# Expert SwiGLU in split float32: one weight tile in six multiplied unsplit for experts with few tokens

## The chip, the cores and the metric

The kernel runs on one core of a Trainium2 chip. The metric is the device time of one execution in microseconds. Before the change it is 1894.84 us, the median of three runs (1893.42 to 1896.1).

## The reference

Two layers of a decoder over 272 tokens (16 meta tokens and 256 of the sequence), all in float32. Each layer has a mixer and a channel mixer; the second layer's channel mixer is the one that matters here: top-2-of-8 experts, each a SwiGLU.

```
logits = t @ router_w + router_b            # (256, 8)
combine = softmax of the top 2, else 0
for e in range(8):
    gate, up = split(t @ w_gu[e])           # 1024 -> 2 x 3584
    out += combine[:, e] * ((silu(gate) * up) @ w_down[e])   # 3584 -> 1024
```

## The kernel before

TensorE has a fast form of float32 product that keeps fewer bits (float32r). For full precision the kernel writes each weight and each activation as a sum of a high part, rounded to float32r, and a low part, the rest, and adds three fast products: high by high, high by low, low by high.

Two thirds of the way, after both mixers and the dense channel mixer, comes the expert stage (`experts`). The tokens of an expert are gathered into a tile `xe` that holds their high and low parts side by side; up to 128 tokens of one expert fit. An expert is worked in 7 steps of 512 hidden columns (56 steps for 8 experts). A step has six units, each one weight tile of 128 x 2048 float32 (1 MB), in the order up 0, up 1, down 0, down 1, up 2, up 3. Up 0 and up 1 make the gate's 512 columns, up 2 and up 3 the up projection's; down 0 and down 1 belong to the step two before. For each unit:

- SP loads the tile into one of 11 buffers (`raw`, line 1228), as soon as the buffer is free.
- ACT copies it, rounded, to `mhi` (`make_high`, line 1241): the high split. There are 3 such buffers. It stands two units ahead of PE in the program.
- DVE subtracts, `raw` minus `mhi`, to `wlo` (`make_low`, line 1250): the low split, one unit ahead of PE, 3 buffers.
- PE multiplies (`products`). An expert with more than 64 tokens (called full here) takes 12 matmuls of 128 x 512: 8 with `mhi` (line 1262, the tokens' high and low parts apart), 4 with `wlo` (line 1264). An expert with up to 64 tokens (called light) has its high and low token parts side by side in one stationary operand of 128 columns (`both`), and takes 8: 4 with `mhi`, 4 with `wlo`. Which arm is taken is a branch on PE alone (line 1271), on a register loaded from the tile `fulli` (line 1289).

Between the units stand small operations. ACT evicts the gate's and the up projection's sums from PSUM (`evict`, line 1294); PE transposes them in quarters (`turn`, line 1300); ACT copies one half of a transposed tile (`second`, line 1304) and DVE adds the other (`total`, line 1308); ACT takes silu of the gate (line 1312), DVE multiplies with the up part (`product`, line 1315), and ACT and DVE split the result for the down projection (`inner`, lines 1326 and 1328). In an expert's second and third step the sums of the expert before are combined into the output (lines 1351, 1353, 1359, 1365), and in odd experts the gathering of the next two experts is strewn in.

The stage runs in the order in which it is written (`manual_schedule`); each engine works its list in order, and the tags that follow `slot` say where each piece stands. The low split of the next step's up 0 stands in slot 5, behind `inner` and ahead of `total` of the gate.

Of the kernel before, what the change touches and what calls it, by code (L numbers as in the profile page):

```python
# [2 lines left out]

# [1 line left out]

# [10 lines left out]
AF = mybir.ActivationFunctionType  # L16
# [45 lines left out]
def rr(ap):  # L62
    return ap.bitcast(F32)
# [38 lines left out]
class Builder:  # L102
# [974 lines left out]
    def some(self, name, shape, dt=F32):  # L1077

        return self.tmp("rt_" + name, shape, dt, bufs=1)
# [125 lines left out]
    def expert_units(self):  # L1205


        self.steps = [(e, j) for e in range(N_EXPERTS) for j in range(NJ)]
        n = len(self.steps)
        self.units = []  # L1210
        for i in range(n):
            self.units += [("up", i, 0), ("up", i, 1)]
            if i > 1:
                self.units += [("down", i - 2, 0), ("down", i - 2, 1)]
            self.units += [("up", i, 2), ("up", i, 3)]
        self.units += [("down", i, q) for i in (n - 2, n - 1) for q in range(2)]
        self.raws, self.high, self.low, self.whole = [], [], [], {}

    def load_unit(self):
        if len(self.raws) == len(self.units):  # L1220
# [10 lines left out]
    def pieces(self, k):  # L1231
        n = 1024 if k == len(self.units) - 1 else 2048
        return [slice(c, c + n) for c in range(0, 2048, n)]

    def make_high(self, k):

        if k < len(self.high) or k >= len(self.units):
            return
        hi = self.hip.tile([P, 2048], F32R, tag="mhi", name=self.name("mhi"))
        for v in self.pieces(k):  # L1240
            self.nc.scalar.activation(hi[:, v], self.raws[k][:, v], AF.Copy)  # L1241
        self.whole[k] = hi
        self.high.append([hi[:, c : c + 512] for c in range(0, 2048, 512)])

    def make_low(self, k):
        if k < len(self.low) or k >= len(self.units):
            return
        lo = self.wp.tile([P, 2048], F32R, tag="w", name=self.name("wlo"))
        for v in self.pieces(k):
            self.nc.vector.tensor_sub(lo[:, v], self.raws[k][:, v], rr(self.whole[k][:, v]))  # L1250
        self.low.append([lo[:, c : c + 512] for c in range(0, 2048, 512)])
        self.load_unit()

    def products(self, k, full, parts, first, last):


        mm = self.nc.tensor.matmul

        def some(cases):
            for i, ((ps, x), hv) in enumerate(zip(parts, self.high[k])):  # L1260
                for c, a in enumerate(cases(x)):
                    mm(ps, a, hv, start=i in first and c == 0, stop=False)  # L1262
            for i, ((ps, x), lv) in enumerate(zip(parts, self.low[k])):
                mm(ps, cases(x)[0], lv, start=False, stop=i in last)  # L1264

        whole = lambda x: (x[:, 0, :], x[:, 1, :])
        both = lambda x: (x.rearrange("p a n -> p (a n)")[:, 0 : 2 * P : 2],)
        if full is None:
            some(whole)
        else:  # L1270
            with self.tc.If(full > 0) as case:
                some(whole)
            with case.Else():
                some(both)

    def experts(self, base, first):

# [3 lines left out]
        nc = self.nc  # L1281
        V, ACT = nc.vector, nc.scalar.activation
        steps = self.steps
        fulls, ps, g, f2, py, y2, sums = {}, {}, {}, {}, {}, {}, {}
        split4 = lambda x: x.rearrange("p (q h n) -> p q h n", h=2, n=HALF)

        def value(e):
            if e < N_EXPERTS:
                fulls[e] = None if base else nc.values_load(
                    self.fulli[0:1, e : e + 1], engines=[mybir.EngineType.PE], min_val=0, max_val=1)  # L1290

        def evict(i, half):
            g[i, half] = self.tmp(f"e{half}", [P, 512], bufs=2 - half)
# [76 lines left out]
        if base == 0:  # L1370
            self.route_end()
        with self.tc.manual_schedule():
            value(0)
            value(1)
            k = 0
            while len(self.raws) < 11:
# [4 lines left out]
            for i, (e, j) in enumerate(steps):  # L1381
# [3 lines left out]
                if j == 2:  # L1385
                    value(e + 1)
# [58 lines left out]
            last = len(steps) - 1  # L1445
# [15 lines left out]
        e = N_EXPERTS - 1  # L1461
# [189 lines left out]
```

## Time and profile before

| | |
|---|---|
| median of three runs | 1894.84 us |
| the profiled execution | 1896.18 us, span 1894.5 us |
| mean granted TensorE clock | 0.984 of full |
| busy: PE, PEld, DVE, ACT, POOL | 94%, 82%, 81%, 68%, 16% |
| DMA | 497.11 MB, mean 262 GB/s |
| first to last expert matmul | 897.8 to about 1874 us |

Busy shares of a whole span mix stages. From about 900 us on the kernel is in the expert stage, where DMA moves 312 to 405 GB/s until the stage's last slice. Which engine ends the waits there has to be read step by step.

### The profile page before, as it was taken

The page shows a single profiled execution, that of the slowest core. Times are in us where ns is not written, and L with a number is a line of the kernel's source. Part 1 is how long each engine was busy: PE and PEld are TensorE (multiplying, and loading weights), DVE is VectorE, ACT ScalarE, POOL GpSimd, SP SyncE. Part 2 cuts the span into 40 slices and gives each one's busy share as a digit, 9 for nine tenths or more (in the row PEclk, how much of TensorE's full clock was granted, in tenths as well). Part 3 has the DMA queues.
Part 4 walks back from the last instruction along what each step waited for, and adds up shares of the span by engine and source line. Part 5 has one row for each costly group of instructions (what it writes and reads, how often), then busy time and mean ns, then how long its engine had stood idle before and what let it go on. Part 6 is the DMA issues. An engine that isn't in the chain of part 4 may idle for free.

```text
span 1894.5 us, 28350 instructions
## 1 busy us (share of the span) xinstructions
PE 1774.5 (94%) x10763; PEld 1545.1 (82%) x10763; DVE 1541.4 (81%) x1700; ACT 1290.0 (68%) x1649; POOL 310.2 (16%) x385
## 2 busy tenths in 40 slices
PE   8999999899999999998999888899999988888996
PEld 7989999899999999997787666677788866666784
DVE  7796665855577967756889999998889899999987
ACT  5564554644456755654788888887777888888774
POOL 6115721600131247423000000000000000000000
PEclk8999999999999999998999999999999999999998
DMA  5445545354454455565799999999899999999990
GB/s 207 147 146 174 176 163 169 106 185 165 155 206 146 153 173 196 185 215 207 279 359 377 360 353 378 390 402 326 312 352 348 363 355 364 394 360 405 366 353 25
DMA packets 74836, 497.11 MB, mean 262 GB/s; under 512 B 9340, under 2 KB 10924, under 8 KB 17324
## 3 DMA queue, kind: packets, MB, share of 16 engines
q1 hardware_dynamic: 69200, 486.64, 69.5%
q10 hardware_dynamic: 5468, 8.15, 1.5%
q8 instruction: 115, 1.88, 0.4%
q14 instruction: 53, 0.43, 0.1%
HBM read 493.65 MB, written 1.10 MB: 261 GB/s over the span
## 4 chain that ended last, share of the span: by engine, by line
PE 65%; DVE 17%; ACT 6%; issue 5%; DMA 5%; POOL 2%; DVEq 0%; ACTq 0%; SPq 0%; POOLq 0%
PE ps_mm L199 12%; PE ps_mm L200 12%; PE ps_mm L201 12%; DVE wlo L1250 11%; PE ps_mm L1262 10%; PE ps_mm L1264 6%; PE ps_acc L1262 4%; DMA raw<-in_up 4%; ACT mhi L1241 4%; PE ps_acc L1264 2%; PE ps_tp L1300 1%; DVE e L1308 1%; PE ps_acc L535 1%; DVE w L173 1%; PE ps_acc L608 1%
## 5 line engine op out<-in xcount | busy, mean ns | idle before, releaser
L1250 DVE TENSOR_TENSOR wlo<-raw,mhi 128x2048 fp32r<-128x2048 f32 x336 | 759.5, 2280 | 56.3 <-ACT mhi L1241 56.3
L1241 ACT ACTIVATE mhi<-raw 128x2048 fp32r<-128x2048 f32 x336 | 633.3, 1908 | 27.3 <-PE ps_acc L1262 17.6
L173 DVE TENSOR_TENSOR w<-raw,w 128x1024 fp32r<-128x1024 f32 (+2 forms) x261 | 322.0, 1234 | 167.1 <-ACT w L172 166.0
L199 PE MATMUL ps_mm<-HL,w 128*128 128x272 f32 (+2 forms) x1344 | 392.5, 292 | 2.0 <-DVE t L394 1.7
L200 PE MATMUL ps_mm<-HL,w 128*128 128x272 f32 (+2 forms) x1344 | 385.3, 287 | 1.1 <-DVE HL L378 1.1
L201 PE MATMUL ps_mm<-HL,w 128*128 128x272 f32 (+2 forms) x1344 | 385.8, 287 | 0.0
L1262 PE MATMUL ps_mm<-mhi,xe 128*128 128x512 f32 x1336 | 354.5, 401 | 1.3 <-issue 1.3
L172 ACT ACTIVATE w<-raw 128x1024 fp32r<-128x1024 f32 (+2 forms) x262 | 267.3, 1020 | 123.9 <-PE ps_mm L201 89.5
L1264 PE MATMUL ps_mm<-wlo,xe 128*128 128x512 f32 x892 | 253.1, 406 | 44.0 <-DVE wlo L1250 43.7
L1262 PEld LDWEIGHTS ps_mm<-mhi,xe 128*128 128x128 f32 x1336 | 250.0, 192 | 53.7 <-issue 4.1
L199 PEld LDWEIGHTS ps_mm<-HL,w 128*128 128x128 f32 x1344 | 253.3, 188 | 5.1 <-issue 3.2
L200 PEld LDWEIGHTS ps_mm<-HL,w 128*128 128x128 f32 x1344 | 253.1, 188 | 1.7 <-DVE HL L378 1.3
L201 PEld LDWEIGHTS ps_mm<-HL,w 128*128 128x128 f32 x1344 | 253.0, 188 | 0.3 <-DVE w L173 0.2
L1264 PEld LDWEIGHTS ps_mm<-wlo,xe 128*128 128x128 f32 x892 | 167.5, 194 | 104.1 <-DVE wlo L1250 72.4
L1262 PE MATMUL ps_acc<-mhi,f 128*128 128x512 f32 x672 | 178.6, 400 | 0.2 <-DVE f L1328 0.2
L1545 POOL TENSOR_TENSOR raw<-raw,gb 128x768 f32<-128x768 f32 x1 | 1.8, 1802 | 985.9 <-ACT raw L1535 985.9
L1262 PEld LDWEIGHTS ps_acc<-mhi,f 128*128 128x128 f32 x672 | 123.5, 190 | 23.8 <-DVE f L1328 0.5
L1294 ACT ACTIVATE e<-ps_mm 128x512 f32<-128x512 f32 x112 | 66.8, 596 | 95.9 <-PE ps_mm L1264 94.2
L1264 PE MATMUL ps_acc<-wlo,f 128*128 128x512 f32 x448 | 126.6, 404 | 4.8 <-DVE wlo L1250 3.4
L1264 PEld LDWEIGHTS ps_acc<-wlo,f 128*128 128x128 f32 x448 | 82.5, 192 | 36.4 <-DVE wlo L1250 21.7
L493 POOL TENSOR_SCALAR seg<-b,ctm 128x16 f32<-128x16 f32 (+3 forms) x96 | 101.0, 1071 | 41.5 <-PE ps_acc L535 20.6
L200 PE MATMUL ps_mm<-YS,w 128*128 128x272 f32 (+1 forms) x256 | 73.2, 286 | 0.0
(355 smaller groups left out, 2477.3 us busy)
## 6 DMA issues: line engine op xcount, KB each, us to landing
raw<-in_up SPq DMA_DIRECT2D x224, 1024.0 KB, 7.0
raw<-in_down SPq DMA_DIRECT2D x110, 1024.0 KB, 7.2
raw<-in_g SPq DMA_DIRECT2D x24, 1024.0 KB, 4.9
raw<-in_q SPq DMA_DIRECT2D x12, 1024.0 KB, 5.4
raw<-in_x SPq DMA_DIRECT2D x12, 1024.0 KB, 4.8
raw<-in_dg SPq DMA_DIRECT2D x11, 1024.0 KB, 4.9
raw<-in_du SPq DMA_DIRECT2D x11, 1024.0 KB, 4.8
raw<-in_dd SPq DMA_DIRECT2D x16, 704.0 KB, 4.0
```

What stands on the lines that cost most here:

```text
L172: pin(nc.scalar.activation(hv, src, AF.Copy))
L173: pin((eng or nc.vector).tensor_sub(lv, src, rr(hv)))
L199: nc.tensor.matmul(ps, h, a, start=first and k == 0, stop=False)
L200: nc.tensor.matmul(ps, h, b, start=False, stop=False)
L201: nc.tensor.matmul(ps, lo, a, start=False, stop=last and k == kn - 1)
L493: nc.gpsimd.tensor_scalar(seg[:, j, c0 : c0 + T - l0], ab[:, j, l0:T], self.ctm[:, ki, hd : hd + 1], 0.0, OP.subtract, OP.min)
L535: nc.tensor.matmul(py[64 * j : 64 * j + 64, l0:T], x4[:, ki, j, :], seg[:, j, c0 : c0 + T - l0], start=ki == 0, stop=ki == 2)
L1241: self.nc.scalar.activation(hi[:, v], self.raws[k][:, v], AF.Copy)
L1250: self.nc.vector.tensor_sub(lo[:, v], self.raws[k][:, v], rr(self.whole[k][:, v]))
L1262: mm(ps, a, hv, start=i in first and c == 0, stop=False)
L1264: mm(ps, cases(x)[0], lv, start=False, stop=i in last)
L1294: ACT(g[i, half], ps.pop((i, half)), AF.Copy)
```

## The change

For experts 0 to 7, in every step but the very first, the unit up 0 becomes conditional on ACT and DVE too. For a full expert all is as before, inside a branch. For a light expert ACT skips the high split and DVE the low split of that unit, and PE multiplies the loaded tile itself, in plain float32, with the same side-by-side stationary operand: 4 float32 matmuls of 128 x 512 in place of 8 fast ones. ACT and DVE therefore load the flag of each expert into a register of their own, as PE did.

```diff
--- before.py
+++ after.py
@@ -1,5 +1,5 @@
 import math
-from contextlib import ExitStack
+from contextlib import ExitStack, nullcontext
 
 import numpy as np
 
@@ -1214,7 +1214,7 @@
                 self.units += [("down", i - 2, 0), ("down", i - 2, 1)]
             self.units += [("up", i, 2), ("up", i, 3)]
         self.units += [("down", i, q) for i in (n - 2, n - 1) for q in range(2)]
-        self.raws, self.high, self.low, self.whole = [], [], [], {}
+        self.raws, self.high, self.low, self.whole, self.fulls = [], [], [], {}, {}
 
     def load_unit(self):
         if len(self.raws) == len(self.units):
@@ -1232,13 +1232,24 @@
         n = 1024 if k == len(self.units) - 1 else 2048
         return [slice(c, c + n) for c in range(0, 2048, n)]
 
+    def direct(self, k):
+
+
+        kind, i, q = self.units[k]
+        e = self.steps[i][0]
+        return kind == "up" and q == 0 and i > 0 and self.fulls[e] is not None
+
+    def if_split(self, k, engine):
+        return self.tc.If(self.fulls[self.steps[self.units[k][1]][0]][engine] > 0) if self.direct(k) else nullcontext()
+
     def make_high(self, k):
 
         if k < len(self.high) or k >= len(self.units):
             return
         hi = self.hip.tile([P, 2048], F32R, tag="mhi", name=self.name("mhi"))
-        for v in self.pieces(k):
-            self.nc.scalar.activation(hi[:, v], self.raws[k][:, v], AF.Copy)
+        with self.if_split(k, mybir.EngineType.Activation):
+            for v in self.pieces(k):
+                self.nc.scalar.activation(hi[:, v], self.raws[k][:, v], AF.Copy)
         self.whole[k] = hi
         self.high.append([hi[:, c : c + 512] for c in range(0, 2048, 512)])
 
@@ -1246,8 +1257,9 @@
         if k < len(self.low) or k >= len(self.units):
             return
         lo = self.wp.tile([P, 2048], F32R, tag="w", name=self.name("wlo"))
-        for v in self.pieces(k):
-            self.nc.vector.tensor_sub(lo[:, v], self.raws[k][:, v], rr(self.whole[k][:, v]))
+        with self.if_split(k, mybir.EngineType.DVE):
+            for v in self.pieces(k):
+                self.nc.vector.tensor_sub(lo[:, v], self.raws[k][:, v], rr(self.whole[k][:, v]))
         self.low.append([lo[:, c : c + 512] for c in range(0, 2048, 512)])
         self.load_unit()
 
@@ -1268,10 +1280,14 @@
         if full is None:
             some(whole)
         else:
-            with self.tc.If(full > 0) as case:
+            with self.tc.If(full[mybir.EngineType.PE] > 0) as case:
                 some(whole)
             with case.Else():
-                some(both)
+                if self.direct(k):
+                    for i, (ps, x) in enumerate(parts):
+                        mm(ps, rr(both(x)[0]), self.raws[k][:, i * 512 : i * 512 + 512], start=i in first, stop=i in last)
+                else:
+                    some(both)
 
     def experts(self, base, first):
 
@@ -1281,13 +1297,14 @@
         nc = self.nc
         V, ACT = nc.vector, nc.scalar.activation
         steps = self.steps
-        fulls, ps, g, f2, py, y2, sums = {}, {}, {}, {}, {}, {}, {}
+        fulls, ps, g, f2, py, y2, sums = self.fulls, {}, {}, {}, {}, {}, {}
         split4 = lambda x: x.rearrange("p (q h n) -> p q h n", h=2, n=HALF)
 
         def value(e):
             if e < N_EXPERTS:
-                fulls[e] = None if base else nc.values_load(
-                    self.fulli[0:1, e : e + 1], engines=[mybir.EngineType.PE], min_val=0, max_val=1)
+                fulls[e] = None if base else {
+                    x: nc.values_load(self.fulli[0:1, e : e + 1], engines=[x], min_val=0, max_val=1)
+                    for x in (mybir.EngineType.PE, mybir.EngineType.Activation, mybir.EngineType.DVE)}
 
         def evict(i, half):
             g[i, half] = self.tmp(f"e{half}", [P, 512], bufs=2 - half)
```

On ACT, in a step in the middle of an expert (here one of expert 0), this stands before, from the eviction of the up part (1294) on; `mhi_11225` is the high split of the next step's up 0:

```order
L1294 ACTIVATE e_1406_11160<-ps_mm_11076 128x512
L1241 ACTIVATE mhi_11162<-raw_10918 128x2048
L1304 ACTIVATE e_1398_11098<-ps_tp_11134 128x4x64
L1271 UNCONDITIONAL_BRANCH
L1241 ACTIVATE mhi_11190<-raw_10945 128x2048
L1271 UNCONDITIONAL_BRANCH
L1241 ACTIVATE mhi_11225<-raw_10979 128x2048
L1326 ACTIVATE f_1416_11227<-e_1398_11098 128x4x2x64
L1304 ACTIVATE e_1406_11160<-ps_tp_11197 128x4x64
```

and this after (line 1294 is now 1311, 1241 is 1252, 1304 is 1321, 1326 is 1343):

```order
L1311 ACTIVATE e_1406_11212<-ps_mm_11132 128x512
L1252 ACTIVATE mhi_11214<-raw_10972 128x2048
L1283 UNCONDITIONAL_BRANCH
L1321 ACTIVATE e_1398_11150<-ps_tp_11186 128x4x64
L1252 ACTIVATE mhi_11242<-raw_10999 128x2048
L1283 UNCONDITIONAL_BRANCH x2
L1250 COMPARE_AND_BRANCH
L1252 ACTIVATE mhi_11277<-raw_11033 128x2048
L1250 UNCONDITIONAL_BRANCH x2
L1343 ACTIVATE f_1416_11280<-e_1398_11150 128x4x2x64
L1321 ACTIVATE e_1406_11212<-ps_tp_11249 128x4x64
```

The order of the work is kept; one high split now lies between a compare-and-branch and its end.

On DVE, at the same kind of place, a step on, before: product (1315), low split of up 3, inner (1328), low split of the next up 0 (`wlo_11445`), total (1308), low split of up 1.

```order
L1315 TENSOR_TENSOR e_1423_11285<-e_1423_11285,e_1406_11160 128x512
L1250 TENSOR_TENSOR wlo_11416<-raw_11132,mhi_11377 128x2048
L1328 TENSOR_TENSOR f_1441_11414<-e_1423_11285,f_1441_11414 128x4x2x64
L1271 UNCONDITIONAL_BRANCH
L1250 TENSOR_TENSOR wlo_11445<-raw_11166,mhi_11412 128x2048
L1308 SCALAR_TENSOR_TENSOR e_1431_11347<-e_1431_11347,rt_all,ps_tp_11384 128x4x64
L1271 UNCONDITIONAL_BRANCH
L1250 TENSOR_TENSOR wlo_11477<-raw_11194,mhi_11443 128x2048
```

and after (1315 is 1332, 1250 is 1262, 1328 is 1345, 1308 is 1325):

```order
L1332 TENSOR_TENSOR e_1423_11335<-e_1423_11335,e_1406_11212 128x512
L1262 TENSOR_TENSOR wlo_11467<-raw_11184,mhi_11427 128x2048
L1250 UNCONDITIONAL_BRANCH
L1345 TENSOR_TENSOR f_1441_11465<-e_1423_11335,f_1441_11465 128x4x2x64
L1260 COMPARE_AND_BRANCH
L1262 TENSOR_TENSOR wlo_11496<-raw_11218,mhi_11462 128x2048
L1260 UNCONDITIONAL_BRANCH x2
L1283 UNCONDITIONAL_BRANCH x2
L1325 SCALAR_TENSOR_TENSOR e_1431_11397<-e_1431_11397,rt_all,ps_tp_11434 128x4x64
L1262 TENSOR_TENSOR wlo_11525<-raw_11246,mhi_11494 128x2048
```

Here too one low split can be jumped over, and nothing else changes places.

On ACT ahead of the first expert, before: the high splits of two units, the split of the tokens (1473), and the copies of the gathered tokens (1179).

```order
L993 ACTIVATE oa<-oa,lt_rs_10032 128x1024
L1241 ACTIVATE mhi_10464<-raw_10016 128x2048
L1241 ACTIVATE mhi_10487<-raw_10018 128x2048
L1473 ACTIVATE xth<-oa 128x1024 x2
L1179 ACTIVATE xe_10315<-ps_tp_10329 128x256
L1179 ACTIVATE xe_10315<-ps_tp_10336 128x256
```

and after:

```order
L993 ACTIVATE oa<-oa,lt_rs_10032 128x1024
L1490 ACTIVATE xth<-oa 128x1024 x2
L1306 TENSOR_LOAD rt_fi
L1306 ISA x2
L1306 TENSOR_LOAD rt_fi
L1306 ISA x2
L1252 ACTIVATE mhi_10504<-raw_10016 128x2048
L1179 ACTIVATE xe_10315<-ps_tp_10329 128x256
```

The two register loads, which need the flag tile `rt_fi`, stand ahead of those two high splits and of the token copies.

## Rows read from the trace of the kernel before

**Rows 1.** Page, part 5: expert matmuls of the high halves (count | busy us, mean ns).
```profile
L1262 PE MATMUL ps_mm<-mhi,xe 128*128 128x512 f32 x1336 | 354.5, 401 | 1.3 <-issue 1.3
...
L1262 PE MATMUL ps_acc<-mhi,f 128*128 128x512 f32 x672 | 178.6, 400 | 0.2 <-DVE f L1328 0.2
```

**Rows 2.** Windows: length, busy us (count) of PE, PEld, DVE, ACT, POOL; clock, DMA.
```profile
1184.38:1247.25 62.87, 53.65 (x225) 39.00 (x224) 61.53 (x41) 54.96 (x48) 0.00 (x0) 1.00 0.99 393
...
1434.87:1505.50 70.63, 70.63 (x324) 57.60 (x323) 62.47 (x42) 55.43 (x48) 0.00 (x0) 1.00 0.96 359
1013.94:1247.25 233.31, 199.21 (x853) 149.84 (x852) 223.92 (x163) 198.85 (x188) 0.00 (x0) 0.99 0.97 375
...
1505.50:1738.58 233.08, 199.19 (x853) 149.87 (x852) 223.90 (x163) 198.84 (x188) 0.00 (x0) 0.99 0.97 373
```

**Rows 3.** Timeline of one light step: start, length, what, [idle before it <- releaser].
```profile
1184.38 1.08 PE L1262 MATMUL ps_mm<-mhi,xe 128*128 128x512 f32 x4
...
1188.99 6.70 DVE L1250 TENSOR_TENSOR wlo<-raw,mhi 128x2048 fp32r<-128x2048 f32 x3 [0.30 <-ACT mhi L1241]
...
1190.66 0.57 ACT L1294 ACTIVATE e<-ps_mm 128x512 f32<-128x512 f32 x1
1191.14 1.91 ACT L1241 ACTIVATE mhi<-raw 128x2048 fp32r<-128x2048 f32 x1
...
1195.60 0.47 DVE L1308 SCALAR_TENSOR_TENSOR e<-e,rt_all,ps_tp 128x256 f32<-128x256 f32 x1
...
1196.11 0.69 DVE L1315 TENSOR_TENSOR e<-e,e 128x512 f32<-128x512 f32 x1
...
1196.72 2.28 DVE L1250 TENSOR_TENSOR wlo<-raw,mhi 128x2048 fp32r<-128x2048 f32 x1
...
1199.06 1.21 PE L1264 MATMUL ps_mm<-wlo,xe 128*128 128x512 f32 x4 [1.07 <-DVE wlo L1250]
1199.52 2.28 DVE L1250 TENSOR_TENSOR wlo<-raw,mhi 128x2048 fp32r<-128x2048 f32 x1
...
1200.10 0.39 PE L1262 MATMUL ps_mm<-mhi,xe 128*128 128x512 f32 x1
```

**Rows 4.** Waits, whole span: who waited for whom, us in total, times, longest.
```profile
PE ps_mm L1264 <- DVE wlo L1250: 43.7, 58, 1.7
```

**Rows 5.** Timeline, PE, one full step.
```profile
1452.86 2.02 PE L1262 MATMUL ps_mm<-mhi,xe 128*128 128x512 f32 x8
...
1455.64 2.02 PE L1262 MATMUL ps_mm<-mhi,xe 128*128 128x512 f32 x8
...
1470.40 0.40 PE L1262 MATMUL ps_mm<-mhi,xe 128*128 128x512 f32 x1
```

**Rows 6.** Timeline, PE, the float32 products at the kernel's end.
```profile
1875.67 3.70 PE L1511 MATMUL ps_mm<-ys,st 128*128 128x512 f32 x8 [0.45 <-ACT ys L1505]
```

**Rows 7.** Timeline, PE, the first light step after a full expert.
```profile
1013.94 1.09 PE L1262 MATMUL ps_mm<-mhi,xe 128*128 128x512 f32 x4
...
1028.21 0.62 PE L1262 MATMUL ps_mm<-mhi,xe 128*128 128x512 f32 x2
```

**Rows 8.** Source lines: branches and register loads (ns, min/median/max); waits: ACT's unexplained idle.
```profile
L1271 PEldq COMPARE_BRANCH  x504: 65/176/441, 897.4 to 1873.5; - x168
...
L1481 DVEq TENSOR_LOAD <-rt_cm x1: 574/574/574, 1888.6 to 1888.6; - x1
...
ACT w L172 <- issue: 19.6, 13, 2.1
```

**Rows 9.** Page, part 6, and SP's waits: loads of expert weights.
```profile
raw<-in_up SPq DMA_DIRECT2D x224, 1024.0 KB, 7.0
...
SPq L1228 <- DVE wlo L1250: 804.2, 320, 13.7
```

**Rows 10.** Timeline, DVE and ACT, before the first expert.
```profile
892.49 0.16 DVE L1156 CAST rt_fi<-rt_all 128x8 int32<-128x8 f32 x1
...
896.49 0.66 ACT L1179 ACTIVATE xe<-ps_tp 128x256 fp32r<-128x256 f32 x2 [9.48 <-PE ps_tp L1176]
```

## The prediction

> **What bounds the kernel now.** The change touches only the expert stage, so I first ask which of its steps it can reach. The page's costliest groups give the matmuls with a high half: 1336 and 672, together 2008 [rows 1]. A light unit has four of them and a full one eight; over 336 units four each make 1344, and the other 664 are about 166 units' second four. So half of the units, 168 or four experts of eight, are full, and four experts are light (some records are missing). The windows show where: in 1013.94 to 1247.25 and in 1505.50 to 1738.58, PE has 853 matmuls in 233 us, the two pairs of light experts, 28 steps [rows 2].
>
> Then I ask what ends the waits in either kind. Four plain light steps lie in 1184.38 to 1247.25: 62.87 us, or 15.72 a step. DVE is busy 61.53 of these (15.38 a step), ACT 54.96 (13.74) [rows 2]. The timeline of one shows DVE almost unbroken, with 0.30 us of waiting for ACT, and PE waiting for low splits: 1.07 us before the low matmuls of up 3 [rows 3]. In the waits by total, PE for the low split is the largest of the stage's PE waits, 43.7 us [rows 4]. So a light step is DVE's. A full step takes 17.54 us (1452.86 to 1470.40) and has 72 matmuls; one unit of twelve takes 2.78, or 0.2317 a matmul, so matmuls alone make 16.68 and transposes and the rest 0.86 [rows 5]. PE is busy all of 70.63 us there, DVE 62.47, some 15.6 a step [rows 2]. A full step is PE's, with 1.9 us to spare on DVE.
>
> **The change, part by part.** In each light step but none of the full ones, DVE loses one low split. Low splits in a row start 2.21 us apart (three in 6.70, the last 2.28) [rows 3], so DVE's own sum falls from 15.38 to 13.17. ACT loses a high split of 1.91, from 13.74 to about 11.9. PE gains: eight fast matmuls, 8 x 0.2317 = 1.85, become four float32 ones. The kernel has four such at its end: they run as eight instructions and take 3.70 us with the tail of the last [rows 6]; I take 3.50 until the next unit's first matmul. PE's own sum for a light step is then 40 x 0.2317 + 0.86 + 3.50 = 13.6. All three sums lie near 13.5, so the step is set by the order in which they hand work on, and I follow that from one up 0 to the next, with the low splits, evictions and waits of rows 3:
>
> - up 0 in float32: 3.50; up 1, eight matmuls with the last one's 0.39 instead of 0.23: 2.01. Nothing is late for them, since the low split of up 1 stands where that of up 0 was.
> - the eviction of the gate's sum starts 0.03 later; the high split behind it 0.48 after that (1190.66 to 1191.14), and lasts 1.91. This is up 2's; the two highs ahead of it start some 1.3 and 3.1 us into the step and are done.
> - 0.03, the low split of up 2, 2.21 until DVE's next (total); 0.51 until product (1195.60 to 1196.11); 0.61 until the low split of up 3 (1196.11 to 1196.72), which lasts 2.28.
> - 0.06 until PE's low matmuls of up 3 (1199.00 to 1199.06), 1.04 from these to the next step's up 0 (1199.06 to 1200.10).
>
> The sum is 14.67 us against 15.72: 1.05 a step, not the 2.21 that DVE saves, since PE's longer unit eats into it and the chain now runs over PE, ACT and DVE in turn. For 28 steps that is 29.4. The combining and gathering steps (the 26 us by which two light stretches of 233 exceed 28 x 15.72 = 440) I count like plain ones; what is added there is DVE and PE work in the same order.
>
> Two of the 28 follow a full expert. The first took 14.27 us (1013.94 to 1028.21), because the splits had been made ahead in the full steps and PE ran without a break [rows 7]. There PE is lengthened by 3.50 - 1.85 = 1.65, with nothing to cover it but what it catches up: between 14.67 and 15.92, I take 15.4. Each loses 1.1 instead of winning 1.05: 4.3 less.
>
> The branches: one compare-and-branch a step on ACT and one on DVE, in 55 steps. The trace has none on these engines; PE's take 0.07 to 0.44 us, 0.18 in the middle [rows 8], and one lies inside the 2.78 of a full unit, where nothing is left for it beside twelve matmuls [rows 5]. On a light step of 14.67 DVE has 1.5 us free, on a plain full step 1.9, so there they cost nothing up to that. In the first three steps of a full expert behind another one DVE is late with gathering and combining; I take 0.2 x 9 = 1.8. From below the price is 0 (in a light step ACT and DVE must see their earlier work done before they go on, which DVE's free time covers). From above I take the longest idle time of ACT that nothing in the trace ends, 2.1 us [rows 8]; that is the third rival. The register loads (DVE's similar one 0.57 us [rows 8]) come once per expert and lie beside a running split. Ahead of the first expert ACT now loads before two high splits: the flags are ready at 892.65, two loads of 0.6 and a split of 1.91 end at 895.8, and ACT idled until 896.49 [rows 10]. If that cover were gone it would cost up to 2 us.
>
> The freed raw tile: its buffer is now released by PE. A load lands 7.0 us after its issue, and is issued when an earlier tile is split, eleven tiles or 29 us before use [rows 9]. The delay of a few us is covered by about 20 us of stock. The light stretch is at 393 GB/s and 99% of DMA [rows 2]; in steps of 14.67 it would need 6.29 MB / 14.67 = 429. What is missing, at most 1.05 us a step or 15 in 14 steps, the stock covers, and full steps, at 359 GB/s, refill it.
>
> Sum: 29.4 - 4.3 - 1.8 = 23.3. The profiled execution took 1896.18, so 1872.9; it lies 1.34 above the median shown, so 1871.5.
>
> **The rivals.** First, DVE's whole saving arrives: the light step falls to the largest own sum, PE's 13.6. Then 28 x 2.1 = 59 us go, and the time is 1836. For it: DVE is busy 98% of a plain light step. Against it: the order, in which up 3's low split waits for product and total.
>
> Second, nothing comes, because the loads are the bound already: 99% of DMA in the light steps, and steps of 15.72 repeated four times. The time stays at 1894. Against it: SP waits 804 us in all for low splits to free a buffer [rows 9], so the loads follow the splits and not the other way round.
>
> Third, slower: a branch on ACT and DVE stops its engine for the time of those unexplained waits, 2.1 us. A light step is then DVE's 13.17 + 2.1 = 15.3, or with the handing on 15.6, and wins 0.1 a step; the full steps lose 0.2 in the 18 plain ones and 2.1 in the nine others, the first light steps 2 each: 3 - 4 - 19 - 4 = 24 lost, 1919. The turning point is about 1.6 us a branch. PE's branches speak against it, but this trace has none on ACT and DVE to go by. The Trainium skill has a rule that points this way (Runtime: NRT & Kernel Launch, section "Instruction fetch mechanics"): a taken branch to code outside the two blocks an engine holds makes it fetch by DMA before it goes on. By that rule, if every one of the 55 met such a fetch, the time would be the 1919; the trace shows no such stop at PE's 504.
>
> **How the numbers follow.** The forecast, a gain by the chain of 8 to 38 us: 0.82. First rival 0.05, second 0.06, third 0.07. The range: with no branch cost and no loss in the first steps 29.4 + 1.8, towards the first rival a little beyond, 1856; with 1.2 us a branch the light step still stays near 14.7, the nine full steps lose 11 and the first steps 3 more, some 10 us of gain are left, 1885, and a little towards the second, 1887. Less than 0.2% either way (4 us) cannot be told from no change here. Faster 0.87, same 0.06, slower 0.07.
>
> **What the profile will show.** Plain light steps of 14.67 (14.2 to 15.1), with up 0's matmuls on line 1288 at 0.43 to 0.46 us an instruction; DVE at about 90% of the step and ACT with gaps ahead of the gate's eviction; PE's wait before up 3's low matmuls still there. Full steps at 17.54. Light stretches of about 222 us in place of 233. If plain full steps grow, or DVE shows idle time that nothing releases around the branch, the third rival holds; if highs wait for loads, the second; if light steps come to 13.6, the order did not matter and the chain was wrong.

## The result, and the profile after

| | before | after |
|---|---|---|
| median | 1894.82 us (4 runs, 1893.42 to 1896.1) | 1873.11 us (4 runs, 1870.55 to 1873.42) |
| profiled execution | 1896.18, span 1894.5 | 1873.42, span 1871.7 |
| ratio, 95% interval | | 0.9881 [0.9869, 0.9894] |

The changed kernel is faster by 21.7 us; 1871.5 was forecast, with 1856 to 1887 as the range.

The starts of the steps' up 0 in the two traces show where the 22.8 us of the span went. The first expert matmul starts 0.55 earlier. Experts 1 and 2 take 221.37 us (before 233.31), experts 5 and 6 220.74 (before 233.08): 24.3 together. The full experts add 0.36, 1.50, -0.02 and 0.06, what follows the start of the last step 0.16 more.

The windows of the kernel after, columns as in [rows 2]: the four plain light steps, the two light pairs, then two plain full steps.

```profile
1176.60:1235.13 58.53, 55.52 (x226) 40.28 (x225) 53.58 (x37) 49.48 (x45) 0.00 (x0) 1.00 1.00 408
1013.76:1235.13 221.37, 209.28 (x854) 152.12 (x853) 196.80 (x150) 175.75 (x175) 0.00 (x0) 0.99 0.97 388
1494.86:1715.60 220.74, 208.95 (x854) 152.08 (x853) 196.75 (x150) 175.67 (x175) 0.00 (x0) 0.99 0.97 390
1459.76:1494.86 35.10, 35.10 (x162) 28.61 (x161) 29.85 (x20) 25.91 (x23) 0.00 (x0) 1.00 0.89 358
```

A plain light step takes 58.53 / 4 = 14.63 us; it was 15.72. No engine fills it: in the four steps DVE is busy 53.58 of 58.53, PE 55.52, ACT 49.48. A full step is PE's as before (35.10 of 35.10 busy, 17.55 a step).

One light step, as in [rows 3], from one up 0 on line 1288 to the next (timeline):

```profile
1191.24 3.59 PE L1288 MATMUL ps_mm<-raw,xe 128*128 128x512 f32 x8
...
1194.27 1.48 PE L1274 MATMUL ps_mm<-mhi,xe 128*128 128x512 f32 x4
1194.39 4.49 DVE L1262 TENSOR_TENSOR wlo<-raw,mhi 128x2048 fp32r<-128x2048 f32 x2 [0.81 <-ACT mhi L1252]
...
1196.73 0.60 ACT L1311 ACTIVATE e<-ps_mm 128x512 f32<-128x512 f32 x1 [0.57 <-PE ps_mm L1276]
...
1197.22 1.91 ACT L1252 ACTIVATE mhi<-raw 128x2048 fp32r<-128x2048 f32 x1
...
1199.16 2.29 DVE L1262 TENSOR_TENSOR wlo<-raw,mhi 128x2048 fp32r<-128x2048 f32 x1 [0.28 <-ACT mhi L1252]
...
1201.37 0.48 DVE L1325 SCALAR_TENSOR_TENSOR e<-e,rt_all,ps_tp 128x256 f32<-128x256 f32 x1
...
1201.88 0.69 DVE L1332 TENSOR_TENSOR e<-e,e 128x512 f32<-128x512 f32 x1
...
1202.49 2.29 DVE L1262 TENSOR_TENSOR wlo<-raw,mhi 128x2048 fp32r<-128x2048 f32 x1
...
1204.83 1.20 PE L1276 MATMUL ps_mm<-wlo,xe 128*128 128x512 f32 x4 [0.75 <-DVE wlo L1262]
...
1205.87 0.59 PE L1288 MATMUL ps_mm<-raw,xe 128*128 128x512 f32 x1
```

Read the brackets: ACT waits for PE before the gate's eviction, DVE for ACT before up 2's low split, PE for DVE before up 3's low matmuls. The work passes round the three engines once a step.

The waits by total, as in [rows 4, 9]: PE's for low splits of the up units fell from 43.7 us to 14.8, and SP now waits partly for the float32 matmuls to free a buffer.

```profile
SPq L1228 <- DVE wlo L1262: 559.7, 247, 13.9
...
SPq L1228 <- PE ps_mm L1288: 121.5, 27, 6.6
...
PE ps_mm L1276 <- DVE wlo L1262: 14.8, 18, 1.3
```

### The profile page after: what moved, and what is told of

Its sections match the earlier page's. It is cut to its first block, busy times and chain, and to the rows that moved or that the text cites. A ratio compares the mean times of both kernels' runs of the same rounds, so it can differ in the third digit from the quotient of the medians.

```text
span 1871.7 us, 28639 instructions
## 1 busy us (share of the span) xinstructions
PE 1792.5 (96%) x10763; PEld 1547.6 (83%) x10763; DVE 1484.5 (79%) x1672; ACT 1240.6 (66%) x1621; POOL 310.0 (17%) x385
## 5 line engine op out<-in xcount | busy, mean ns | idle before, releaser
L1262 DVE TENSOR_TENSOR wlo<-raw,mhi 128x2048 fp32r<-128x2048 f32 x308 | 697.2, 2280 | 81.0 <-ACT mhi L1252 80.9
L1252 ACT ACTIVATE mhi<-raw 128x2048 fp32r<-128x2048 f32 x308 | 582.3, 1908 | 36.8 <-PE ps_mm L1274 13.0
L1274 PE MATMUL ps_mm<-mhi,xe 128*128 128x512 f32 x1224 | 330.2, 406 | 0.2
L1274 PEld LDWEIGHTS ps_mm<-mhi,xe 128*128 128x128 f32 x1224 | 227.5, 191 | 55.2 <-issue 11.5
L1276 PE MATMUL ps_mm<-wlo,xe 128*128 128x512 f32 x780 | 216.5, 399 | 15.1 <-DVE wlo L1262 14.8
L1276 PEld LDWEIGHTS ps_mm<-wlo,xe 128*128 128x128 f32 x780 | 147.7, 192 | 55.3 <-DVE wlo L1262 25.6
L1288 PE MATMUL ps_mm<-raw,xe 128*128 128x512 f32 x224 | 101.0, 594 | 0.8 <-DMA raw<-in_down 0.6
```

Source lines behind the costliest of these rows:

```text
L1288: mm(ps, rr(both(x)[0]), self.raws[k][:, i * 512 : i * 512 + 512], start=i in first, stop=i in last)
```

## The experiments

Every kernel here was timed beside the kernel before on the same chip; the ratio is to that. Diffs are against the changed kernel. Expectations stand as they were on record before the runs. Where nothing else is said, the windows quoted are of the four plain light steps of expert 2.

**The branches by themselves.** Both arms of the new branches split, and PE takes the fast products, so only branches and register loads are added to the kernel before (`cut` makes the split).

```diff
-        with self.if_split(k, mybir.EngineType.Activation):
+        self.two_arms(k, mybir.EngineType.Activation, cut)   # If: cut(), Else: cut()
...
-        with self.if_split(k, mybir.EngineType.DVE):
+        self.two_arms(k, mybir.EngineType.DVE, cut)
...
-                if self.direct(k):
+                if False:
```

> Branches alone: ACT and DVE branch on the flag around up 0's splits, but both arms hold the split, and PE multiplies split tiles as before. Chain theory (branches are free, since both traces show 38 and 47 ns a piece): within 3 us of before, 1892 to 1898, light plain steps 15.7, full plain 17.55. Rival, that branches hold their engines up for some tenths: light steps longer by what a branch costs, since DVE is 98% busy there; 0.2 us would give 16 in light steps and 1900 or more.

Measured: 1896.08 us, ratio 1.0007 [0.9998, 1.0016].

```profile
1182.26:1245.13 62.87, 53.64 (x226) 38.97 (x224) 61.54 (x41) 54.96 (x48) 0.00 (x0) 1.00 1.00 394
```

The same 62.87 us as before, and plain full steps still take 17.55. The branches cost nothing that this can tell; the third rival falls. Their own rows in the changed kernel say why (source lines; ns, min/median/max; there are 82 records on each engine where I had counted 55 branches):

```profile
L1250 ACTq COMPARE_BRANCH  x82: 34/38/50, 906.0 to 1815.3; - x82
```
```profile
L1260 DVEq COMPARE_BRANCH  x82: 43/47/63, 904.4 to 1817.9; - x82
```

A jump over a split is not in this kernel, since both arms hold one. In the changed kernel's light step above, DVE has 0.15 us of idle time behind such a jump: `inner` ends at 1205.38 and total starts at 1205.53. That is off the chain of the step that is followed below.

**PE's part alone.** PE multiplies up 0 unsplit, but ACT and DVE make both splits all the same.

```diff
-        return self.tc.If(self.fulls[...][engine] > 0) if self.direct(k) else nullcontext()
+        return nullcontext()
```

> PE's part alone: a light expert's up 0 is multiplied in float32, but ACT and DVE go on making its splits, which nobody reads there. Chain theory: the step is DVE's again and PE's 1.7 us more hide in its waits: plain light steps 15.7 to 15.8, only the first light step after a full expert longer by 1.2; time 1894 to 1900. Rival, PE's addition always counts: 17.4 a step, time 1940.

Measured: 1899.75 us, ratio 1.0034 [1.0021, 1.0047].

```profile
1185.17:1248.02 62.85, 58.17 (x225) 39.36 (x224) 61.52 (x41) 54.92 (x48) 0.00 (x0) 1.00 0.98 390
```

PE is busier by 4.5 us in four steps (58.17 against 53.65 [rows 2]) and the steps are as long as before: PE's extra hides while DVE is full (61.52 of 62.85 us). The first light step after a full expert, where PE has no slack, grows to 15.43. So the gain comes from what ACT and DVE leave out, and the loss of the first steps from PE.

**A shorter float32 unit.** Two of the four float32 matmuls are left out.

```diff
-                    for i, (ps, x) in enumerate(parts):
+                    for i, (ps, x) in enumerate(parts[:2]):
```

> The change, but of up 0's four float32 matmuls in a light expert only two are made (half of that unit's products are left out), so PE spends about 1.8 us on the unit, as with eight fast ones. Chain theory: with PE's piece 1.7 shorter the chain over up 0 and the gate's eviction goes, and the step falls only to what DVE and ACT hand on without it, 14.2 (0.45 less, not 1.7); the first light step comes back to 14.3; time about 1862. Rival, PE's own sum is the bound: steps fall by the whole 1.7 to 12.9, time about 1825. Rival, the loads are the bound (430 GB/s): steps stay at 14.63, time 1872.

Measured: 1860.12 us, ratio 0.9819 [0.9805, 0.9832].

```profile
1172.36:1229.44 57.08, 50.89 (x210) 36.52 (x208) 53.23 (x37) 49.09 (x45) 0.00 (x0) 1.00 1.01 415
```

14.27 us a step, though PE has about 1.7 us less to do (four instructions 0.43 us apart). ACT's timeline in one of these steps shows what is late instead:

```profile
1187.85 3.71 ACT L1252 ACTIVATE mhi<-raw 128x2048 fp32r<-128x2048 f32 x2
1191.45 0.59 ACT L1311 ACTIVATE e<-ps_mm 128x512 f32<-128x512 f32 x1
```

The gate's eviction has no wait for PE ahead of it now (0.57 us of it in the changed kernel); it starts as ACT's two high splits end. The float32 unit is thus a link of the chain, as the prediction had it, but by 0.36 us only: behind it ACT's own list is next. The first light step is back at 14.26, so its loss is the length of that unit.

**Another unit unsplit: up 1, up 3, up 2.** One number changes in each.

```diff
-        return kind == "up" and q == 0 and i > 0 and ...
+        return kind == "up" and q == 1 and i > 0 and ...   # then 3, then 2
```

> The same change for up 1 instead of up 0: the same number of splits left out, the same PE work. Chain theory: almost nothing is won, plain light steps stay at 15.7, since the low split of up 0 still stands ahead of total, silu waits for total, the high split of down 0 stands behind silu, and DVE then has to wait for it in the time in which it made up 1's low split; time 1890 to 1897. Rival, sums count (DVE's saving less PE's extra): the same gain as with up 0, steps of 14.6, time 1873.

Measured for up 1: 1900.21 us, ratio 1.0031 [1.0019, 1.0044]. The steps stayed at 15.71 as expected, the total missed what was expected by 3 us: the two first light steps take 15.44 each, as with up 0, and one full step (20.70, before 19.07) holds a stretch at the lower clock. The window, then DVE's timeline in a light step:

```profile
1185.21:1248.05 62.84, 56.65 (x226) 39.95 (x224) 52.71 (x37) 49.55 (x45) 0.00 (x0) 1.00 0.98 391
```
```profile
1184.64 2.28 DVE L1262 TENSOR_TENSOR wlo<-raw,mhi 128x2048 fp32r<-128x2048 f32 x1
1186.84 0.47 DVE L1325 SCALAR_TENSOR_TENSOR e<-e,rt_all,ps_tp 128x256 f32<-128x256 f32 x1
1189.81 6.69 DVE L1262 TENSOR_TENSOR wlo<-raw,mhi 128x2048 fp32r<-128x2048 f32 x3 [2.50 <-ACT mhi L1252]
```

and ACT's in the same step:

```profile
1187.35 0.63 ACT L1329 ACTIVATE e<-e 128x512 f32<-128x512 f32 x1 [1.34 <-DVE e L1325]
1187.89 3.70 ACT L1252 ACTIVATE mhi<-raw 128x2048 fp32r<-128x2048 f32 x2
```

DVE's saved 2.2 us turn into a wait of 2.50. The low split of up 0 still stands ahead of total, silu on ACT waits for total, and the high split that DVE needs next stands behind silu. Leaving out up 0 takes the low split from ahead of total; leaving out up 1 takes one from behind it, where it bought nothing.

> The same change for up 3, the step's last unit. Chain theory: no low split stands between product and inner any more and nothing on the way to the eviction is lengthened ahead of the gate's eviction; plain light steps of about 14.4, and the steps that combine an expert's sums shorter by 0.8 than with up 0; time 1864 to 1870. Rival, sums count: as with up 0, 1873. Rival, the loads are the bound: not under 14.63 a step.

Measured for up 3: 1865.15 us, ratio 0.9851 [0.9836, 0.9866]; plain steps 14.48, first light steps 15.03.

```profile
1170.93:1228.84 57.91, 57.20 (x227) 39.74 (x225) 52.77 (x37) 47.72 (x44) 0.00 (x0) 1.00 1.01 415
```

> The same change for up 2. Chain theory: total and product come 2.2 us earlier, plain light steps about 14.4, like up 3 (14.47) and less than up 0 (14.63); time 1863 to 1868. Rival, sums count: no difference to up 0 beyond noise, 1873.

Measured for up 2: 1876.21 us, ratio 0.9902 [0.9887, 0.9917]. The plain steps came as expected, the total did not.

```profile
1179.03:1236.95 57.92, 56.68 (x225) 40.01 (x224) 52.78 (x37) 47.59 (x44) 0.00 (x0) 1.00 1.01 414
```

Up 2 and up 3 give the same plain step, and the totals lie 11 us apart. The difference is in the odd experts, which gather tokens for the next two: experts 1 and 5 take 119.6 and 118.2 us with up 2, 113.6 and 113.4 with up 3, 115.3 and 114.8 with up 0.

**Up 2 with an earlier high split.** The high split of down 0 goes ahead of the eviction and silu of the step before.

```diff
-        return kind == "up" and q == 0 and i > 0 and ...
+        return kind == "up" and q == 2 and i > 0 and ...
...
                     if slot == 0 and i:
+                        self.make_high(k + 2)
                         evict(i - 1, 1)
                         silu(i - 1)
```

> As e5, and at the head of each step ACT makes the high split of down 0 before the eviction and silu instead of behind them. Chain theory: DVE no longer waits for that split, and with up 2 in float32 no chain is longer than PE's own sum; plain light steps come down to 13.5 to 13.7 until the stock of loaded tiles is used up, since 1 MB in 2.28 us would be 460 GB/s and the most seen in any 50 us is 419; then waits for loads appear. Time 1846 to 1858. Rival, nothing but the sum of DVE's and PE's work counts, and e5 has it already: no difference to e5.

Measured: 1862.41 us, ratio 0.9826 [0.9813, 0.984].

```profile
1175.82:1230.29 54.47, 54.47 (x225) 40.61 (x224) 53.20 (x37) 48.16 (x45) 0.00 (x0) 1.00 1.01 419
```

Here a plain step is 13.62 us and PE is busy in all of it: the 13.6 that the prediction gave as PE's own sum, reached once the order no longer holds the work back. DMA moves 419 GB/s meanwhile, and the weight loads hold up no engine for more than 1.3 us in all, so the second rival (loads are the bound) is out too. The total was above what was expected, again by the gathering steps. PE's timeline in one of them:

```profile
1099.74 0.43 PE L1194 MATMUL ps_tp<-rt_id,sel 128*128 128x128 f32 x2 [2.18 <-DVE sel L1193]
1101.27 0.69 PE L1194 MATMUL ps_tp<-rt_id,sel 128*128 128x128 f32 x2 [1.10 <-DVE sel L1193]
1101.95 2.07 PE L1274 MATMUL ps_mm<-mhi,xe 128*128 128x512 f32 x4
```

PE waits 2.18 us for DVE's selection matrices, and the four matmuls behind take 2.07 us in place of 1.09, since the granted clock falls to its lower level there: 0.53 over these 6.8 us (a window of this kernel).

```profile
1101.30:1108.10 6.80, 6.80 (x19) 5.41 (x20) 5.90 (x6) 0.98 (x2) 0.00 (x0) 0.53 0.78 276
```

These waits come to 8.8 us in all here and in the kernel with up 2 alone, and to 8.7 before; in the changed kernel they come to 5.7 and the longest is 1.1, with up 3 to 5.6 (waits by total, of this kernel, of the changed one and of before). So up 2 unsplit leaves them as they were, and up 0 and up 3 shorten them; why was not taken apart.

```profile
PE ps_tp L1194 <- DVE sel L1193: 8.8, 7, 2.2
```
```profile
PE ps_tp L1194 <- DVE sel L1193: 5.7, 7, 1.1
```
```profile
PE ps_tp L1194 <- DVE sel L1193: 8.7, 7, 2.1
```

The clock has a share in the 11 us between up 2 and up 3. With up 3 the granted clock is 1.00 all through experts 1 and 5; with up 2 alone it is 0.50 for 6.8 us of expert 1 (window below) and 3.4 us of expert 5. As an estimate, 10.2 us at half speed are up to 5.1 us lost.

```profile
1101.80:1108.60 6.80, 6.40 (x18) 5.05 (x18) 5.86 (x8) 1.33 (x3) 0.00 (x0) 0.50 0.72 251
```

**The same earlier high split with up 0.** One line is added to the changed kernel.

```diff
                     if slot == 0 and i:
+                        self.make_high(k + 2)
```

> The change as it is, and ACT makes down 0's high split before the eviction and silu, which takes away the longest wait of DVE in a plain light step, 0.81 us at down 0's low split. Chain theory: that wait is not on the chain, which runs over PE's up 0 and up 1 to the gate's eviction; plain light steps stay at 14.6, time 1869 to 1876, no change beyond noise to the changed kernel. Rival, DVE's idle time is what is left to win: steps of 13.9, time 1855.

Measured: 1870.03 us, ratio 0.9869 [0.9854, 0.9884]; plain steps 14.63 (58.54 us for four), as in the changed kernel. DVE's early wait of 0.81 us is not what the step hangs on. The intervals of the two ratios overlap, so the 3 us in the total are not shown to be a gain; between the two traces 1.6 us of the difference lie in the step that has the lower clock in the changed kernel (20.66) and not here (19.07).

**Two units unsplit, up 0 and up 2.**

```diff
-        return kind == "up" and q == 0 and i > 0 and ...
+        return kind == "up" and q in (0, 2) and i > 0 and ...
```

> Two units of a step unsplit for light experts, up 0 and up 2: DVE loses two splits a step, PE gains 3.3 us. Chain theory: PE's own sum, 32 x 0.2317 + 0.86 + 7.0 = 15.2 us, is the bound; steps of 15.1 to 15.3, so less is won than with one unit, 1875 to 1882. Rival, DVE's work is what counts: steps fall below 14, 1855.

Measured: 1889.01 us, ratio 0.9967 [0.9955, 0.9979].

```profile
1184.04:1244.85 60.81, 60.81 (x226) 40.64 (x224) 46.22 (x34) 43.58 (x41) 0.00 (x0) 1.00 1.00 404
```

Now PE is the bound: 60.81 of 60.81, 15.20 us a step, as expected of the steps. The total was not: the first light steps take 17.01, the gathering ones about 18.2. A second unit off DVE costs more on PE than it gives.

**The best of both.** Odd experts, which gather, leave up 3 unsplit; even ones leave up 2 unsplit and have the earlier high split.

```diff
-        return kind == "up" and q == 0 and i > 0 and ...
+        return kind == "up" and q == (3 if e % 2 else 2) and i > 0 and ...
...
                     if slot == 0 and i:
+                        if e % 2 == 0:
+                            self.make_high(k + 2)
```

> A version put together from the runs: in experts with an odd number, among whose steps the gathering is strewn, up 3 is left unsplit and the order is as it was; in the even ones up 2, with down 0's high split first. If the steps keep the times that they had in those two runs (expert 1 with up 3: 113.6 us, expert 2 with up 2 and early high: 100.2, and the same for 5 and 6), the time is 4.5 us less per pair than with up 3 alone: 1854 to 1860. Rival, the loads: two light experts in 214 us need 84 MB at 393 GB/s, and the stock of tiles gives out: 1862 or more.

Measured: 1857.88 us (1854.06 to 1859.58), ratio 0.98 [0.9787, 0.9814]: 15 us below the changed kernel's 1873.11 and the fastest of all here, inside what was expected. No engine waits more than 1.9 us in all for a load of weights, so the rival of the loads did not come. Experts 1 and 5 take 113.7 and 114.8 us, experts 2 and 6 101.1 and 101.2, and PE's waits for the selection matrices are back at 5.7 in all.

```profile
1171.58:1226.06 54.48, 54.48 (x226) 40.61 (x224) 53.23 (x37) 47.41 (x44) 0.00 (x0) 1.00 1.01 417
```

## Why the prediction was right

**The chain of a light step: 14.67 worked out, 14.63 measured.** The links, from the timeline above: up 0 and up 1 to the gate's eviction 5.49 (5.54 in the prediction; up 1's first matmul starts 3.03 after up 0's and not 3.50, but up 1 is slower to run, and the two together fit); to the high split 0.49 (0.48); the high and the hand-on 1.94 (1.94); low split to total 2.21 (2.21), to product 0.51 (0.51), to the low split of up 3 0.61 (0.61), to PE's low matmuls 2.34 (2.34), to the next up 0 1.04 (1.04). Such links add up to the step whatever sets it; that this chain sets it was shown from two sides: a shorter float32 unit shortened it, and only until ACT's own list ended later; and the order of e.g. up 1 against up 0, with the same work left out, decided between nothing and 1.09 us a step.

**The first rival, all of DVE's saving.** It did not come, for the reason given: the sums alone do not set the step. The bound it named, 13.6, is real, and up 2 unsplit with the earlier high split reaches it (13.62).

**The first light steps.** 15.4 was taken between 14.67 and 15.92; both took 15.43. The rows answer to [rows 7]: PE runs from 1013.76 to 1029.19 without a break (busy all of the 15.43). From up 0's start to the low matmuls of up 1 it takes 4.36 us, before 2.79 (last row), so up 0 costs 1.57 more there, and 0.41 of that came back. That some would come back was in the prediction; how much was a guess between two bounds, and it landed.

```profile
1013.76 3.59 PE L1288 MATMUL ps_mm<-raw,xe 128*128 128x512 f32 x8
...
1018.12 1.09 PE L1276 MATMUL ps_mm<-wlo,xe 128*128 128x512 f32 x4
...
1029.19 0.59 PE L1288 MATMUL ps_mm<-raw,xe 128*128 128x512 f32 x1
```
```profile
1016.73 1.09 PE L1264 MATMUL ps_mm<-wlo,xe 128*128 128x512 f32 x4
```

**The other 14 light steps, counted like plain ones.** Before they took 124.75 and 124.51 us in the two pairs, after 118.15 and 117.55: 0.97 a step where 1.05 was counted. The mean held. Single steps did not: the second of a pair came 2.3 to 2.4 shorter, the third 0.5 to 0.7 longer. And part of the mean is the clock. Before, four stretches at the lower clock lie in these 14 steps, after only two. One of the four is in the third step of expert 2 (16.25 us, clock 0.89); with branches alone the same step has none and takes 15.57 (windows of before, then of that kernel).

```profile
1168.13:1184.38 16.25, 15.10 (x60) 11.95 (x61) 15.62 (x13) 13.06 (x11) 0.00 (x0) 0.89 0.87 324
```
```profile
1166.69:1182.26 15.57, 13.84 (x60) 10.78 (x61) 15.54 (x13) 13.21 (x11) 0.00 (x0) 1.00 0.92 344
```

**The branches: 1.8 priced, nothing found.** With branches alone the nine steps that the price stood on agree with before to 0.1 us each; another full step grew by 1.6, and in it lies a stretch at the lower clock. In the changed kernel such a stretch fell in one of the nine (20.66 us against 19.07), so the sum came out near by chance: the full experts did lose 1.9 us, 1.6 of it there and not to branches. The price of the branches is the one term of the sum that was wrong in kind. The trace shows the stretch, first in the kernel after, then the same place before, with the same wait and no fall of the clock (timelines of PE, and a window of after):

```profile
1269.32 0.73 PE L1376 MATMUL ps_tp<-sel,st 128*128 128x512 f32 x2 [1.54 <-DVE e L1325]
1270.13 3.55 PE L1274 MATMUL ps_mm<-mhi,xe 128*128 128x512 f32 x8
```
```profile
1270.13:1274.57 4.44, 4.43 (x13) 3.50 (x13) 4.44 (x4) 3.20 (x3) 0.00 (x0) 0.62 0.65 269
```
```profile
1281.44 0.73 PE L1359 MATMUL ps_tp<-sel,st 128*128 128x512 f32 x2 [1.54 <-DVE e L1308]
1282.34 2.08 PE L1262 MATMUL ps_mm<-mhi,xe 128*128 128x512 f32 x8 [0.16 <-issue]
```

Eight matmuls take 3.55 us in place of 2.08 while the granted clock over the stretch is 0.62. In the kernel before, the same wait of 1.54 was followed by full speed; why it falls in one run and not in the other was not settled.

**The freed tile and the loads.** Light steps draw 408 GB/s (429 was worked out as the need), and a load of an up tile lands after 7.8 us instead of 7.0 [rows 9]. Waits of the float32 matmuls for a load come to 0.6 us in all, and no other engine's wait in the expert stage ends with a load, so the stock covered the rest.

```profile
L1288 PE MATMUL ps_mm<-raw,xe 128*128 128x512 f32 x224 | 101.0, 594 | 0.8 <-DMA raw<-in_down 0.6
```
```profile
raw<-in_up SPq DMA_DIRECT2D x224, 1024.0 KB, 7.8
```

**Ahead of the first expert.** The register loads take less than the 0.6 us assumed, 0.28 in the middle on ACT (0.48 at most), and the first expert matmul did not come later but 0.55 us earlier. That this half microsecond comes from the change is not shown: ACT still waits 0.69 us for PE ahead of the token copies.

```profile
L1306 ACTq TENSOR_LOAD <-rt_fi x9: 278/284/482, 891.9 to 1635.9; - x9
```

## What to carry to other kernels

Where three engines hand work round and none is full for the whole step, do not take the saving of the busiest one: follow the links from one repeat to the next with the durations of the trace, put the new lengths in, and see what is late next. Which of several equal pieces of work is dropped can matter more than that one is dropped, so look for the piece that stands ahead of what the next engine waits for (here, up 0 ahead of total, against up 1 behind it). Count the steps that carry extra work apart from the plain ones: they decided between up 2 and up 3, whose plain steps were equal.

## What was not expected of the hardware

- A compare-and-branch on ACT and DVE takes 0.038 and 0.047 us in the middle, against 0.176 on PE's queue, and one a step on each made no measurable difference (1.0007).
- Behind waits of PE of 1.1 to 2.3 us the granted clock sometimes drops to its lower level (1.2 GHz) for some us; the one quoted cost 1.6 us. Among the experts the trace of before has four such stretches, that of the changed kernel three, that with up 0 and up 2 none. They come and go between kernels whose code at that place is the same, which makes totals differ by a few us where plain steps agree to 0.02.
